# The up product of an MLP by seven half-size products (Strassen's scheme), one token block at a time, in a one-core encoder step on Trainium2

## The chip, the cores and the metric

The kernel runs on one core of one Trainium2 chip. A core has a matrix engine (TensorE, in the profile PE, with its weight loads as PEld), a vector engine (VectorE, DVE), an engine for functions of one input (ScalarE, ACT), a slower general engine (GpSimd, POOL) and an engine that issues DMAs (SyncE, SP). Each runs its own instruction stream in order and waits for the others by semaphores. The metric is the device time of one execution in microseconds (us); the time of a kernel is the median of its runs.

## What is computed

One step of a one-layer streaming encoder: 2048 prompt tokens and 32 sample tokens, model width 1024. A normed input goes through one projection, two kinds of attention, an output projection, then an MLP with squared ReLU and a gated per-layer input; last a norm. The part that matters here, from the reference:

```python
def ffn_ple(h, p, g_mlp, w_up, w_down, w_ple_gate, w_ple_proj):
    c = rmsnorm(h, g_mlp)
    h = h + jnp.square(jax.nn.relu(c @ w_up)) @ w_down
    return h + jax.nn.sigmoid(h @ w_ple_gate) * (p @ w_ple_proj)
...
        hp = hp + merge(oa, ob, subln_g[i], out_norm_b[i], w_out[i], lam_init)
        hp = ffn_ple(hp, p_prompt[i], g_mlp[i], w_up[i], w_down[i], w_ple_gate[i], w_ple_proj[i])
```

`w_up` is 1024 x 4096, `w_down` 4096 x 1024, `w_ple_gate` 1024 x 1024, `w_ple_proj` 256 x 1024, all float32.

## The kernel before

**Tokens.** They are held transposed (features on the 128 partitions, tokens along the free side) in four blocks of 512; the 32 sample tokens join block 3, which so has 544 and is computed in two halves of 272 (`SUBS`), since a matmul takes at most 512 columns.

**Split operands.** Every float32 operand `x` of a product is split into a rounded `hi` and a rest `lo = x - hi` (`split`, L167: ACT copies to `hi`, POOL or DVE subtracts for `lo`), and `mm3` (L191) makes three matmuls for each 128 x 128 weight tile: hi x hi, hi x lo, lo x hi. POOL's part goes through `pool_tt` (L148), which cuts a tensor into instructions of at most 256 columns. `wunit` (L178) loads 128 x 1024 weights into a raw tile and splits them whole; three such units are buffered.

**MLP of blocks 2 and 3.** `mlp` (L1033) runs 16 chunks of 256 hidden features. For a chunk, `mlp_up` (L973) loads two units of `w_up`, and for each of the two 128-feature tiles and each block makes 8 x 3 matmuls over the 1024 inputs into one PSUM bank, then ReLU, square and a split into `uh`, `ul` (two ACT passes L996 and L997, `hi` on ACT, `lo` on POOL). `mlp_down` (L1001) multiplies the outputs of the chunk before with two units of `w_down` and adds each PSUM result to `h` on DVE (L1031). Both blocks share each weight unit. Per chunk TensorE makes 48 up matmuls of 512 columns and 96 of 272, and as many down matmuls.

**Around it.** Blocks 0 and 1 go first. The second part of `run` (from L1316) then runs: `outproj(2)`; `outproj(3)` with `cnorm(2)` (the normed and split MLP input of block 2, L925) woven in; `gate(0)` (L1048) with `cnorm(3)` woven in; the final norm of block 0 behind the first chunk of the MLP; the MLP of blocks 2 and 3; `gate(2)`; `gate(3)` with `final(2)` in it; and `final(3)` (L1106), whose last half closes the run. A gate splits `h` into eight tiles (`hu` or `hH`, `hL`), makes for each of eight output tiles 24 gate matmuls (`gps`) and 6 projection matmuls (`pps`) per block of columns, computes a sigmoid on ACT with a subtraction on POOL, multiplies on DVE and adds to `h` on POOL.

**Order.** The kernel is written in Python generators that are woven by hand (`weave`, `drain`, `next`); this sets priorities. A planner then lists the instructions of each engine by these priorities and a model of their times, so that the matmuls of up and down products stand interleaved in TensorE's stream. Buffers are tiles of pools with a number of slots per name; an instruction that needs a slot waits for its last reader.

## Time and profile before

| | |
|---|---|
| median of 3 runs | 3222.55 us |
| lowest and highest run | 3216.17 and 3224.60 us |
| the profiled execution, whole | 3219.67 us |
| its span on the core | 3217.9 us |
| its mean granted TensorE clock | 0.981 |

The span runs from the first to the last instruction of the program; the rest of the execution's time lies around it. In the profile, a row of a group has the line, the engine, the operation, what it writes and reads, the shapes and the count; then busy time and the mean duration of one; then the idle time of that engine just before these instructions and what ended it. A row of the timeline has the start in us from the beginning of the span and the duration; in square brackets stands the idle time before it. Matmuls overlap in the pipeline, so their durations are longer than the distance between two starts.

### The profile page before, as it was taken

To read this page: it belongs to the slowest core of one execution; us is meant where nothing else is said; L and a number is where in the kernel's file an instruction comes from. 1 tells how busy PE (TensorE), PEld (TensorE's weight loads), DVE (VectorE), ACT (ScalarE), POOL (GpSimd) and SP (SyncE) were. 2 spreads that over 40 slices of the span, in tenths; PEclk is the share of its full clock that TensorE was granted. 3 is DMA by queue.
4 is the path that set the end of the run, shared out by engine and by line. 5 is a ranking of instruction groups with operands and counts; after the bars stand their busy time and mean duration, and the time that the engine had idled before them with its cause. 6 is when DMAs were issued, how large, how long until landed. Compare 5 with 4: busy or idle time off the path is not lost. (4 is left out here: it accounts for less than half of the span.)

```text
span 3217.9 us, 51221 instructions
## 1 busy us (share of the span) xinstructions
PE 3073.5 (96%) x17881; PEld 2698.6 (84%) x17881; DVE 1560.4 (48%) x3969; ACT 1724.7 (54%) x3819; POOL 1704.1 (53%) x2530
## 2 busy tenths in 40 slices
PE   8998989999999998999999999999999999999998
PEld 7787877899987787878788888888789999999988
DVE  5156774544465554676755656526432223223335
ACT  6256775766675674766666666444542322322255
POOL 4466546434345544565655545687954433333387
PEclk9998999999999999999999999999999999999999
DMA  8787768976787645555564543548431111111122
GB/s 265 238 245 222 204 193 235 258 221 203 204 247 221 202 126 144 151 154 149 154 180 126 141 120 107 158 124 259 145 111 44 45 47 47 46 47 47 59 86 87
DMA packets 503273, 487.90 MB, mean 152 GB/s; under 512 B 36924, under 2 KB 392576, under 8 KB 503016
## 3 DMA queue, kind: packets, MB, share of 16 engines
q1 hardware_dynamic: 503016, 484.64, 51.5%
q8 instruction: 141, 2.31, 0.3%
q14 instruction: 116, 0.95, 0.1%
HBM read 378.52 MB, written 109.95 MB: 152 GB/s over the span
## 5 line engine op out<-in xcount | busy, mean ns | idle before, releaser
L165 POOL TENSOR_TENSOR wl<-wr,wh 128x256 fp32r<-128x256 f32 x936 | 689.1, 768 | 466.2 <-ACT wh L170 454.2
L170 ACT ACTIVATE wh<-wr 128x1024 fp32r<-128x1024 f32 x338 | 357.0, 1057 | 590.8 <-PE dps L196 291.5
L1031 DVE TENSOR_TENSOR h<-h,dps 128x512 f32<-128x512 f32 (+1 forms) x640 | 373.8, 586 | 584.8 <-PE dps L197 567.8
L155 POOL TENSOR_TENSOR wl<-wr,wh 128x256 fp32r<-128x256 f32 x416 | 308.5, 772 | 359.7 <-ACT wh L170 354.2
L195 PE MATMUL dps<-uh,wh 128*128 128x512 f32 (+1 forms) x1280 | 458.4, 358 | 21.9 <-ACT wh L170 7.8
L196 PE MATMUL ups<-cL,wh 128*128 128x512 f32 (+1 forms) x1280 | 451.4, 353 | 2.0 <-POOL cL L155 1.8
L195 PE MATMUL ups<-cH,wh 128*128 128x512 f32 (+1 forms) x1280 | 451.7, 353 | 0.5 <-DVE h L1031 0.4
L196 PE MATMUL dps<-ul,wh 128*128 128x512 f32 (+1 forms) x1280 | 451.1, 353 | 0.0
L197 PE MATMUL ups<-cH,wl 128*128 128x512 f32 (+1 forms) x1280 | 451.0, 352 | 0.0
L197 PE MATMUL dps<-uh,wl 128*128 128x512 f32 (+1 forms) x1280 | 450.5, 353 | 0.0
L195 PEld LDWEIGHTS dps<-uh,wh 128*128 128x128 f32 x1280 | 241.9, 189 | 57.6 <-DVE h L1031 12.8
L155 POOL TENSOR_TENSOR ul<-relu,uh 128x136 fp32r<-128x136 f32 (+1 forms) x320 | 198.0, 640 | 170.9 <-ACT uh L170 169.7
L197 PEld LDWEIGHTS dps<-uh,wl 128*128 128x128 f32 x1280 | 241.3, 189 | 33.3
L196 PEld LDWEIGHTS ups<-cL,wh 128*128 128x128 f32 x1280 | 241.6, 189 | 32.8 <-POOL cL L155 2.0
L195 PEld LDWEIGHTS ups<-cH,wh 128*128 128x128 f32 x1280 | 241.6, 189 | 32.8 <-DVE h L1031 1.6
L197 PEld LDWEIGHTS ups<-cH,wl 128*128 128x128 f32 x1280 | 241.6, 189 | 29.4
L196 PEld LDWEIGHTS dps<-ul,wh 128*128 128x128 f32 x1280 | 242.0, 189 | 26.7
L195 PE MATMUL qps<-aH,wh 128*128 128x512 f32 (+1 forms) x640 | 230.0, 359 | 5.7 <-DVE ql L455 4.2
L196 PE MATMUL qps<-aL,wh 128*128 128x512 f32 (+1 forms) x640 | 228.6, 357 | 0.0
L197 PE MATMUL qps<-aH,wl 128*128 128x512 f32 (+1 forms) x640 | 228.3, 357 | 0.0
L612 PE MATMUL s<-ka,q 128*128 128x512 f32 (+3 forms) x768 | 188.1, 348 | 20.9 <-DMA ka<-kS 8.5
L626 ACT ACTIVATE e<-s,nm 128x512 f32<-128x512 f32 (+3 forms) x256 | 154.8, 609 | 75.6 <-DVE nm L618 64.5
(233 smaller groups left out, 7160.8 us busy)
## 6 DMA issues: line engine op xcount, KB each, us to landing
wr<-w_up SPq DMA_DIRECT2D x96, 512.0 KB, 4.1
wr<-w_down SPq DMA_DIRECT2D x96, 512.0 KB, 3.8
wr<-w_in SPq DMA_DIRECT2D x74, 512.0 KB, 4.7
q<-qS SPq DMA_DIRECT2D x128, 256.0 KB, 5.6
v<-vSa SPq DMA_DIRECT2D x64, 512.0 KB, 3.7
ka<-kS SPq DMA_DIRECT2D x32, 512.0 KB, 7.9
wr<-w_out SPq DMA_DIRECT2D x32, 512.0 KB, 4.9
wr<-w_ple_gate SPq DMA_DIRECT2D x32, 512.0 KB, 4.2
```

The lines of the kernel that those rows point to most:

```text
L155: nc.gpsimd.tensor_tensor(out[:, sl], a[:, sl], b[:, sl], op=op)
L165: nc.gpsimd.tensor_tensor(out[:, sl], a[:, sl], b[:, sl], op=op)
L170: nc.scalar.activation(hi, raw, AF.Copy)
L195: nc.tensor.matmul(ps, lh, rh, start=start and i == 0, stop=False)
L196: nc.tensor.matmul(ps, lh, rl, start=False, stop=False)
L197: nc.tensor.matmul(ps, ll, rh, start=False, stop=stop and i == n - 1)
L612: nc.tensor.matmul(s, q[:, m, hl, P * qi : P * qi + nr], kt[:, m, k0 - kb : k0 - kb + n], start=hl == 0, stop=hl == 1)
L626: nc.scalar.activation(dst, src, AF.Exp, bias=nmx, accum_out=z[:nr, m, bi : bi + 1])
L1031: nc.vector.tensor_tensor(hv, hv, ps, op=ALU.add)
```

## The change

For blocks 2 and 3 the up product of a chunk is taken as a product of 2 x 2 blocks: the weights are cut into two halves of hidden features (128 each) and two halves of inputs (512 each), the tokens into two halves (256 each, or 272 in block 3). Seven half-size products of sums of these parts replace the eight (the Winograd form of Strassen's scheme). `cparts` builds the seven token-side operands once per block (seven hi/lo pairs, in four steps); `mlp7` builds the seven weight-side operands per chunk and adds the products up on DVE, ACT and POOL. `mlp7` takes one block, so the MLP runs as 16 chunks for block 2 and then 16 for block 3; each loads and splits its weights itself. `gate(2)` now stands between them, with `cparts(3)` woven in; `cparts(2)` is woven into `gate(0)`, where `cnorm(3)` was. Weights after block 1 are split in pieces of 512 columns with eight piece buffers (`pieces`). At the end, the two POOL steps of the last two output tiles of `gate(3)` go to DVE, and in the last norm half of the scalings go to ACT. Cut to its core:

```diff
+class Parts:
+    def __init__(self, tiles, per):
+        self.tiles, self.per = tiles, per
+    def __getitem__(self, idx):
+        k = idx[1]
+        return self.tiles[k // self.per][(idx[0], k % self.per) + tuple(idx[2:])]
...
@@ wunit
+        if self.pieces is not None:
+            n = shape[0] // 2
+            parts = []
+            for x in range(2):
+                parts.append(self.piece([n] + shape[1:]))
+                self.split(*parts[x], raw[:, n * x : n * x + n], hi_eng, lo_eng)
+            return tuple(Parts([p[i] for p in parts], n) for i in range(2))
...
+    def piece(self, shape):
+        return [r.tile([P] + shape, F32R, name="piece") for r in self.pieces]
...
+    def cparts(self, b, wk, cs, out, r):
...
+        names = ("b11", "b21", "t2", "t1", "t3", "b22", "t4")
+        ops = {x: [cs.tile([P, 4, 272], F32R, tag="cs", name="cs")[:, :, :m] for _ in range(2)] for x in names}
+        for k in range(4):
+            c = []
+            for i in range(2):
+                tmp = wk.tile([P, BLK], F32, tag="tmp", bufs=self.nt, name="tmp")[:, :n]
+                kk = k + 4 * i
+                self.dma(tmp, self.hS[:, kk, t0 : t0 + n])
+                nc.vector.scalar_tensor_tensor(
+                    tmp, tmp, self.g_mlp[:, kk : kk + 1], r, op0=ALU.mult, op1=ALU.mult
+                )
+                c.append((tmp[:, :m], tmp[:, m:]))
+            (b11, b12), (b21, b22) = c
...
+            parts(("b11", "pool"), ("b21", "dve"), ("b22", "pool"))
+            nc.vector.tensor_tensor(b22, b22, b12, op=ALU.subtract)
+            nc.vector.tensor_tensor(b12, b12, b11, op=ALU.subtract)
+            nc.vector.tensor_tensor(b11, b22, b11, op=ALU.add)
+            nc.vector.tensor_tensor(b21, b21, b11, op=ALU.subtract)
+            parts(("t2", "dve"), ("t1", "pool"), ("t3", "dve"), ("t4", "pool"))
+            yield
...
+    def mlp7(self, b, h, ops, wk, up, mm, md):
...
+        def downs(ch, us):
+            for dh in range(2):
+                wh, wl = self.wunit(
...
+                for d in range(4):
+                    for s0, sn in SUBS[b]:
+                        ps = md.tile([P, 512], F32, tag="mm", name="dps")[:, :sn]
...
+                        nc.vector.tensor_tensor(hv, hv, ps, op=ALU.add)
+                    yield
...
+        def prod(out, more, w, x):
+            ps = banks.tile([P, 512], F32, name="ups")[:, :m]
+            self.mm3(ps, [(w[0][:, k], w[1][:, k], ops[x][0][:, k], ops[x][1][:, k]) for k in range(4)])
+            if more is None:
+                nc.scalar.activation(out, ps, AF.Copy)
+            else:
+                nc.vector.tensor_tensor(out, more, ps, op=ALU.add)
+            return out
+
+        def square(u, r, lo_eng):
+            nc.scalar.activation(r, r, AF.Relu)
+            nc.scalar.activation(r, r, AF.Square)
+            self.split(*u, r, "act", lo_eng)
...
+        for ch in range(DFF // (2 * P)):
...
+            self.split(*w["a11"], a11)
+            self.split(*w["a12"], a12)
+            s2 = self.sums.tile([P, 4, P], F32, tag="s2", bufs=1, name="s2")
+            nc.vector.tensor_tensor(a21, a11, a21, op=ALU.subtract)
+            nc.vector.tensor_tensor(s2, a22, a21, op=ALU.subtract)
+            nc.vector.tensor_tensor(a11, s2, a11, op=ALU.add)
+            nc.vector.tensor_tensor(a12, a12, s2, op=ALU.subtract)
+            for x, t, e in (("s2", s2, "dve"), ("s1", a11, "pool"), ("s3", a21, "dve"), ("s4", a12, "pool"), ("a22", a22, "dve")):
+                self.split(*w[x], t, "act", e)
...
+            t1 = prod(tmp("t1", m), None, w["a11"], "b11")
+            prod(c11, t1, w["a12"], "b21")
+            u2 = prod(tmp("u2", m), t1, w["s2"], "t2")
+            next(prev, None)
+            t5 = prod(tmp("t5", m), None, w["s1"], "t1")
+            next(prev, None)
+            u3 = prod(tmp("u3", m), u2, w["s3"], "t3")
+            self.pool_tt(u2, u2, t5, ALU.add)
+            self.pool_tt(c22, u3, t5, ALU.add)
+            next(prev, None)
+            next(prev, None)
+            prod(c12, u2, w["s4"], "b22")
+            square(us[0], r0, "dve")
+            next(prev, None)
+            prod(c21, u3, w["a22"], "t4")
+            square(us[1], r1, "pool")
+            drain(prev)
+            prev = downs(ch, us)
+            yield
+        drain(prev)
...
@@ gate
-                    self.pool_tt(sg, sm, sg, ALU.subtract)
+                    end = b == 3 and d >= 6
+                    if end:
+                        nc.vector.tensor_tensor(sg, sm, sg, op=ALU.subtract)
+                    else:
+                        self.pool_tt(sg, sm, sg, ALU.subtract)
...
-                    self.pool_tt(hv, hv, sg, ALU.add)
+                    if end:
+                        nc.vector.tensor_tensor(hv, hv, sg, op=ALU.add)
+                    else:
+                        self.pool_tt(hv, hv, sg, ALU.add)
@@ final
-                nc.vector.tensor_copy(yns[c0, q][:tn], yp[:tn])
+                if phased:
+                    nc.vector.tensor_tensor(yns[c0, q][:tn], yp[:tn], self.gf[:tn, :512], op=ALU.mult)
+                else:
+                    nc.vector.tensor_copy(yns[c0, q][:tn], yp[:tn])
...
-                nc.vector.scalar_tensor_tensor(yn[:tn], src[:tn], r, g, op0=ALU.mult, op1=ALU.mult)
+                if phased and q == 0:
+                    nc.scalar.activation(yn[:tn], src[:tn], AF.Copy, scale=r)
+                else:
+                    nc.vector.scalar_tensor_tensor(yn[:tn], src[:tn], r, g, op0=ALU.mult, op1=ALU.mult)
@@ run
+            wpx.close()
+            self.wp = opened(top, "wp4", 6)
+            wx = opened(top, "wx", 2, side="right")
+            self.sums = wx
+            self.pieces = [Rings(*[(self.wp, t)] * 3, (wx, t)) for t in ("wh", "wl")]
...
+            cs = Sized(opened(top, "cs", 14), None)
+            ops = {}
+            h = hload(hh, BLK, 0)
+            g = self.gate(0, h, up, None, md, wk)
             next(g)
...
-            r = self.colnorm(acc[3][0], 3, 1.0 / D, wk, mm, "mm", None)
-            weave(g, self.cnorm(3, wk, act, cn, r), 1)
+            r3 = self.colnorm(acc[3][0], 3, 1.0 / D, wk, mm, "mm", None)
+            weave(g, self.cparts(2, wk, cs, ops, r2), 1)
             f = self.final(0, h, up, fk, mm)
-            st = {b: (hload(hh, BLK, b),) + cn[b] for b in HALVES[1]}
-            m = self.mlp(HALVES[1], st, wk, up, mm, md)
+            h = hload(hh, BLK, 2)
+            m = self.mlp7(2, h, ops[2], wk, up, mm, md)
             next(m)
             drain(f)
             drain(m)
-            drain(self.gate(2, st[2][0], up, act, md))
-            g = self.gate(3, st[3][0], up, act, md)
-            f = self.final(2, st[2][0], up, fk, mm)
-            for _ in range(4):
+            g = self.gate(2, h, up, None, md, wk)
+            next(g)
+            weave(g, self.cparts(3, wk, cs, ops, r3), 1)
+            f = self.final(2, h, up, fk, mm)
+            h = hload(hh, BLK, 3)
+            m = self.mlp7(3, h, ops[3], wk, up, mm, md)
+            next(m)
+            drain(f)
+            drain(m)
+            g = self.gate(3, h, up, cs, md)
+            f = self.final(3, h, up, fk, mm, md)
+            for _ in range(5):
                 next(g)
...
```

More of the change, by code (lines that the diff above doesn't have):

```diff
@@ L139, in __init__ @@
         self.nt = 3
+        self.pieces = None
     def dma(self, dst, src):
@@ L941, in cnorm, with parts @@
             yield
+    def cparts(self, b, wk, cs, out, r):
+        nc = self.nc
+        n, t0 = BN[b], 512 * b
+        m = n // 2
+        names = ("b11", "b21", "t2", "t1", "t3", "b22", "t4")
+        ops = {x: [cs.tile([P, 4, 272], F32R, tag="cs", name="cs")[:, :, :m] for _ in range(2)] for x in names}
+        out[b] = ops
+        for k in range(4):
[9 more added lines that the diff above has]
+            (b11, b12), (b21, b22) = c
+            raw = {"b11": b11, "b21": b21, "b22": b22, "t3": b22, "t1": b12, "t2": b11, "t4": b21}
+            def parts(*which):
+                for x, e in which:
+                    self.split(ops[x][0][:, k], ops[x][1][:, k], raw[x], "act", e)
+            parts(("b11", "pool"), ("b21", "dve"), ("b22", "pool"))
[5 more added lines that the diff above has]
+            yield
     def colnorm(self, *args):
@@ L1055, in gate @@
                 self.dma(pT[i][k][:, :n], self.pS[:, i, k, t0 : t0 + n])
-        if wk is None:
+        if wk is None and act.aw is None:
+            hc = [act.tile([P, 4, 272], F32R, tag="cs", name="hc").rearrange("p a b -> p (a b)") for _ in range(8)]
+            hH, hL = [[hc[4 * i + k // 2][:, BLK * (k % 2) : BLK * (k % 2) + n] for k in range(8)] for i in range(2)]
+        elif wk is None:
             hH = act.tile([P, 8, act.aw], F32R, tag="act", name="hH")
```

63 lines of the change are left out of this document (50 added, 13 removed).

## The prediction

> **What bounds the kernel now.** I read the page first, then the last third of the span in stretches, then the timeline of TensorE and of POOL in it.
>
> ```profile
> span 3217.9 us, 51221 instructions
> PE 3073.5 (96%) x17881; PEld 2698.6 (84%) x17881; DVE 1560.4 (48%) x3969; ACT 1724.7 (54%) x3819; POOL 1704.1 (53%) x2530
> PE   8998989999999998999999999999999999999998
> POOL 4466546434345544565655545687954433333387
> ```
>
> TensorE never rests from the 30th slice on, and POOL is at three to four tenths in the MLP of blocks 2 and 3 but at eight or nine around it (the gates). By stretches (columns: length; busy us and instructions of PE, PEld, DVE, ACT, POOL; clock; DMA):
>
> ```profile
> 2264.00:2327.00 63.00, 59.16 (x245) 46.68 (x246) 31.34 (x36) 34.35 (x55) 58.78 (x80) 0.97 0.45 137
> 2327.00:2362.00 35.00, 32.62 (x194) 29.15 (x193) 11.85 (x17) 18.54 (x38) 30.81 (x45) 0.95 0.29 92
> 2362.00:3079.00 717.00, 716.03 (x4447) 649.90 (x4446) 213.06 (x417) 207.12 (x365) 281.62 (x442) 1.00 0.17 53
> 3079.00:3200.00 121.00, 120.67 (x764) 109.65 (x763) 46.43 (x90) 68.39 (x148) 102.83 (x165) 1.00 0.28 88
> ```
>
> The rows are gate(0), the MLP's start, the rest of the MLP, and gates 2 and 3. The MLP is bound by TensorE alone (0.97 us idle in 717), so fewer matmul columns there shorten the run, as long as the other engines keep up.
>
> **What a matmul costs.** Busy times overlap, so I use the distance between starts: in a run of 512-column matmuls, one of 272 and one of 256 (value projection, early in the kernel).
>
> ```profile
> 3086.24 0.40 PE L195 MATMUL gps<-hH,wh 128*128 128x512 f32 x1
> ...
> 3089.93 0.39 PE L196 MATMUL gps<-hL,wh 128*128 128x512 f32 x1
> ```
> ```profile
> 2601.24 0.29 PE L195 MATMUL ups<-cH,wh 128*128 128x272 f32 x1
> ...
> 2603.99 0.28 PE L196 MATMUL ups<-cL,wh 128*128 128x272 f32 x1
> ```
> ```profile
> 51.79 0.28 PE L195 MATMUL vps<-wh,aH 128*128 128x256 f32 x1
> ...
> 54.09 0.28 PE L197 MATMUL vps<-wh,aL 128*128 128x256 f32 x1
> ```
>
> 3.69 us over 16 steps is 0.231 us; 2.75 over 22 is 0.125; 2.30 over 20 is 0.115 (its first five steps are 0.12). As a check, one third at 0.231 and two thirds at 0.125 give 0.160 us; the MLP row has 717/4447 = 0.161. So halving a 512-column matmul, each half with its own weight load, costs almost nothing. I take 0.1165 for 256 columns, bounds 0.115 and 0.120.
>
> The page "TensorE: Matmul & The Clock Gate" of the Trainium skill, section "Back-to-back issue gap", speaks against the change: it gives a sustained spacing of about 131 ns at 512 columns and 81 at 128. An estimate between them is 98 ns at 256, so 1344 x 98 - 768 x 131 ns would add 31 us in block 2 instead of removing 20. The rows above contradict it at both widths.
>
> **The terms.** Up product of block 2, 16 chunks: before 16 x 48 = 768 matmuls of 512, 177.4 us; after 16 x 7 x 4 x 3 = 1344 of 256, 156.6: -20.8 (bounds -16 and -23). Block 3: before 16 x 96 = 1536 of 272, after 1344 of 272: 192 x 0.125 = -24.0. Down products, gates and transposes keep their matmuls. **Sum on TensorE: -44.8.**
>
> What is added is vector work: each block now loads and splits its own weights, the up weights become seven pieces, and products are summed outside PSUM. Prices:
>
> ```profile
> L155 POOL TENSOR_TENSOR wl<-wr,wh 128x256 fp32r<-128x256 f32 x132 | 93.2, 737 | 173.7 <-ACT wh L170 173.7
> L155 POOL TENSOR_TENSOR ul<-relu,uh 128x136 fp32r<-128x136 f32 x128 | 58.4, 477 | 33.1 <-ACT uh L170 33.1
> L170 ACT ACTIVATE uh<-relu 128x272 fp32r<-128x272 f32 x64 | 27.6, 432 | 2.0
> L170 ACT ACTIVATE uh<-relu 128x512 fp32r<-128x512 f32 x32 | 20.2, 632 | 1.0
> L1031 DVE TENSOR_TENSOR h<-h,dps 128x272 f32<-128x272 f32 x254 | 110.6, 438 | 50.0 <-PE dps L197 38.0 <-DMA h<-hS 3.8
> L1031 DVE TENSOR_TENSOR h<-h,dps 128x512 f32<-128x512 f32 x128 | 88.0, 688 | 452.6 <-PE dps L197 452.4
> ```
>
> Per chunk of block 2, TensorE needs 84 x 0.1165 + 48 x 0.231 = 20.9 us. ACT: 11 pieces, 6 passes of the two squares at 0.632, two copies at 0.43: 11.6. POOL: lo halves of four up pieces and four down pieces (two instructions each), two sums, two for a square's lo half: 20 x 0.737 = 14.7. DVE: 8 x 0.688 down sums, 5 x 0.438 product sums, and eight 512-wide instructions with both inputs in SBUF (four weight sums, four lo halves). Those eight decide, because they and POOL get in each other's way (the down sums, with one input in PSUM, leave POOL at 737 ns above):
>
> ```profile
> 2212.07 4.73 POOL L165 TENSOR_TENSOR wl<-wr,wh 128x256 fp32r<-128x256 f32 x4
> ```
> ```profile
> 2311.62 5.61 DVE L937 SCALAR_TENSOR_TENSOR tmp<-tmp,g_mlp_s,r 128x544 f32<-128x544 f32 x1 [0.73 <-DMA tmp<-hS]
> 2317.95 0.72 DVE L176 TENSOR_TENSOR cL<-tmp,cH 128x544 fp32r<-128x544 f32 x1 [0.72 <-ACT cH L170]
> ```
>
> Four POOL instructions, one DVE instruction beside each, took 4.73 us instead of 4 x 0.737: each DVE instruction adds 0.45 to POOL. The other way a DVE instruction waited 5 us behind POOL's; behind it would stand the product and down sums, whose eight PSUM banks TensorE wants back after eight groups of 12 x 0.1165 or 6 x 0.231 = 1.4 us, so 11 us of cover. The Trainium skill ("SBUF — State Buffer", section "Who interferes with whom") says that a DVE instruction with two SBUF inputs contends with one of GpSimd that reads SBUF, and that the shared pair is an exclusive lock. The trace agrees on the contention, but with 0.45 us of delay and not the full 0.72.
>
> So POOL's path is 14.7 + 8 x 0.45 = 18.3 us per chunk against 20.9 (88%). Block 3: 16 x 0.737 + 4 x 0.477 + three thirds of a 544-wide row (about 0.575 each, between the two rows) = 15.4, with 3.6 of delay 19.0 against (84 + 96) x 0.125 = 22.5. DVE is 7.7 + 8 x 1.17 = 17.1 us with its waits. Everything fits, but the eight piece buffers for eleven pieces per chunk leave little slack: the first down pieces of a chunk get their buffers as the last chunk ends, and TensorE wants them 3 products, 4.2 us, later; two pieces need about 0.63 + 4 x 0.737 = 3.6. The **stall in the steady chunks** is unknown: 0 as in the present MLP, or up to 8 x (0.72 - 0.45) = 2.2 us each if POOL waits out each DVE instruction whole. I take 0.3, near the row of the MLP, which is the nearest: **+10** over 32 chunks.
>
> **The stage borders.** Building the seven operand parts (cparts) is woven into gate(0) and now also into gate(2), which stood free. A gate is 240 x 0.231 = 55.4 us of TensorE and about 80 POOL instructions (40 weight lo's, 8 for h, 32 of sigmoid and sum): 59.0 us. Gate(2) gets 32 of 136 columns (15.3) and from DVE 12 wide and 28 half instructions (12 x 0.45 + 28 x 0.23 = 11.8): 86 us. Work ahead in the eight pieces is 16 instructions (11.8), and the last two columns' sums (5.9) can trail: 68 - 55.4 = 13 us of stall, where the row of gates 2 and 3 shows 0.3 now: **+13** (bounds 4, if the planner spreads the sums into the MLP, and 28). Gate(0): 59.0 + 16 x 0.737 + 11.8 = 82.6, less 17.7, less 55.4: 9.5, where the first two stretch rows show 6.2 idle, and the MLP's start offers less cover (9.8 us of products in chunk 0 instead of 23): **+6** (bounds 0 and 14). Gate(2)'s lo halves share 20 tiles with the MLP's outputs, of which the last four come free at its end: **+1**. The operands' DMAs and the second reading of the up and down weights cost nothing while the DMA share is 0.17; doubled it stays below the 0.45 of gate(0), and a load lands in a fifth of a chunk; uncovered, each would cost those 4 us:
>
> ```profile
> wr<-w_up SPq DMA_DIRECT2D x96, 512.0 KB, 4.1
> ```
>
> **The tail.** After the last gate matmul:
>
> ```profile
> 3200.25 0.29 PE L197 MATMUL gps<-hH,wl 128*128 128x272 f32 x1
> ...
> 3201.98 0.91 POOL L155 TENSOR_TENSOR sig<-sm,sig 128x136 f32<-128x136 f32 x2 [0.93 <-ACT sig L1085]
> ...
> 3204.02 0.90 POOL L155 TENSOR_TENSOR h<-h,sig 128x136 f32<-128x136 f32 x2 [1.14 <-DVE sig L1101]
> ```
> ```profile
> 3208.49 0.75 DVE L1143 SCALAR_TENSOR_TENSOR yn<-yn,rsy,gf 128x512 f32<-128x512 f32 x1
> ...
> 3214.44 0.73 DVE L1143 SCALAR_TENSOR_TENSOR yo<-yp,rsy,gf 32x512 f32<-32x512 f32 x1
> ```
>
> The two POOL steps go to DVE: 2 x (0.9 - 0.44) = -0.9. The ten scalings of 0.66 in a row become five on DVE and five on ACT side by side: -3.3. **-4** together (0 if ACT waits for DVE's lock, -5 at best).
>
> **Sum:** -44.8 - 4 + 10 + 13 + 6 + 1 = -19. The profiled execution took 3219.67 us (its span and 1.8 around it), 2.9 under the median of the runs; so 3201 from it, 3204 from the median. I predict **3202**.
>
> **Rivals.**
>
> *The shared path binds the chunk (slower).* If each of the eight DVE instructions holds POOL for its full 0.72 us, POOL's path is 14.7 + 5.8 = 20.5 us of 20.9, and the order of waits does the rest: late lo halves hold the piece buffers, the next raw loads and the down products. For it: the 5.6 us wait above, and DVE at 17 us. Against it: gate(0) ran 63 us with POOL at 58.78 busy and TensorE lost 3.8. Without steady stalls the sum is -29, so the sign turns at 0.9 us per chunk; at 2 us it is +35: 3256.
>
> *A draw.* Stalls of 0.6 to 1.2 us per chunk, with borders as forecast, eat the gain: -29 + 32 x 0.6 to -29 + 32 x 1.2 is -10 to +9, about 3222.
>
> *The borders cost nothing.* The order of instructions pushes POOL's gate sums into the MLP, as now at 2327 (30.81 of 35 us POOL busy while TensorE ran 32.62), and steady chunks run full: -44.8 - 4 + 4 = -45: 3176. Against it: the MLP that follows has no longer 60% of POOL free, but 12%.
>
> *The matmul count saves nothing*, since a half-width matmul is bound by its weight load: the 256-column run speaks against it. At 0.132 per matmul block 2 gains nothing: -19 + 21: 3222.
>
> **How the numbers follow.** Forecast 0.48, draw 0.10, shared path 0.27, free borders 0.13, weight load 0.02. About 0.3% (9.7 us) is what a measurement here can tell from no change: the forecast is faster but for its upper edge (0.44 of 0.48), free borders are faster; that is 0.57. Same: 0.04 + 0.10 + 0.02 = 0.16. Slower: 0.27. The forecast's own range is 3186 to 3216 (steady 0 to 0.5 us, borders within their bounds); the range to both rivals is 3174 to 3256.
>
> **What would show it.** Right: up products of block 2 start every 0.115 to 0.12 us, the two MLPs have TensorE idle under 1% with POOL near 75 to 80% busy, gate(2) is 10 us or more longer than 55 with TensorE waiting for the lo halves of weights or operand parts, and the tail from the last gate matmul is 13 to 14 us instead of 17.6. Wrong: PE waits for POOL or DVE in every chunk (shared path), a gate(2) without idle time, or a pitch of 0.13 and more. The prediction falls if either MLP has over 15 us of TensorE idle.

## The result, and the profile after

| | before | after |
|---|---|---|
| median of 12 runs each | 3218.45 us | 3225.85 us |
| lowest and highest | 3213.31 and 3224.60 us | 3217.70 and 3229.67 us |
| the profiled execution, its span | 3219.67, 3217.9 us | 3225.84, 3224.0 us |
| mean granted clock | 0.981 | 0.976 |

After over before is 1.002 (95% interval 1.001 to 1.0029): the changed kernel is 0.2% slower, some 6 us, where 0.5% faster was forecast. The page of the changed kernel, cut to four of its rows, shows that TensorE did get less to do:

```profile
PE 3036.1 (94%) x18265; PEld 2691.8 (83%) x18265; DVE 1854.1 (58%) x4436; ACT 1885.7 (58%) x4166; POOL 1959.8 (61%) x2782
PE   8998989999999999999999999999989999799998
POOL 4466556433345444665555545678977778877675
PEclk9998999999999999999999999999999999899999
```

PE's busy time fell from 3073.5 to 3036.1 us, 37 less, and the span still grew by 6.1. The unbroken row of nines from the 30th slice on has two dents now, an 8 in the 30th slice and a 7 in the 35th, and in the latter the granted clock has one too. POOL went from three or four tenths to seven or eight. The stretches show which stages the dents are in. The columns are the length, then busy us and instructions of PE, PEld, DVE, ACT and POOL, the clock, the DMA share and GB/s. Before, the start of `outproj(2)`, the MLP of both blocks, and gates 2 and 3:

```profile
2158.80:2160.60 1.80, 1.80 (x11) 1.45 (x9) 0.00 (x0) 1.58 (x3) 0.72 (x2) 1.00 0.40 121
...
2326.90:3079.30 752.40, 749.05 (x4642) 679.41 (x4641) 225.07 (x433) 225.96 (x403) 312.83 (x488) 1.00 0.18 55
3079.30:3200.50 121.20, 120.87 (x765) 109.85 (x764) 46.33 (x89) 68.09 (x148) 102.89 (x165) 1.00 0.28 88
```

After, the start of `outproj(2)` (from the last gate matmul of block 1 to the first `ops`), both output projections, gate(0), block 2's MLP, gate(2) with block 3's MLP, gate(3), and the tail:

```profile
2157.80:2169.70 11.90, 5.26 (x25) 3.77 (x23) 4.90 (x8) 5.22 (x13) 3.07 (x5) 0.75 0.84 264
2169.70:2272.90 103.20, 97.88 (x590) 87.54 (x591) 47.64 (x74) 45.55 (x92) 86.46 (x113) 0.98 0.78 233
2272.90:2336.00 63.10, 58.15 (x246) 46.66 (x245) 50.21 (x61) 36.81 (x77) 59.10 (x69) 0.97 0.32 97
2336.00:2695.10 359.10, 346.30 (x2145) 309.52 (x2144) 235.31 (x375) 188.00 (x350) 275.07 (x346) 0.99 0.36 112
2695.10:3145.30 450.20, 426.32 (x3152) 413.44 (x3151) 300.23 (x558) 224.93 (x421) 348.93 (x483) 0.97 0.32 99
3145.30:3206.80 61.50, 61.50 (x494) 61.50 (x493) 19.69 (x43) 34.76 (x84) 45.23 (x84) 1.00 0.13 35
3206.80:3224.00 17.20, 3.64 (x31) 2.99 (x29) 6.56 (x15) 9.01 (x24) 0.00 (x0) 0.74 0.36 130
```

The MLPs with their gates took 752.4 + 121.2 = 873.6 us and take 359.1 + 450.2 + 61.5 = 870.8. The whole scheme of seven products thus bought 2.8 us, and the start of `outproj(2)` alone costs 10.1 more than before (11.9 against 1.8). Inside the two MLPs, away from their starts, all is as it should be. Stretches of the changed kernel: the start of block 2's MLP, its steady part, gate(2), the start of block 3's MLP, its steady part:

```profile
2336.00:2400.00 64.00, 51.20 (x334) 45.95 (x333) 49.06 (x85) 34.78 (x82) 52.74 (x64) 0.92 0.44 151
2400.00:2690.00 290.00, 290.00 (x1792) 259.45 (x1791) 181.15 (x283) 148.91 (x261) 217.92 (x278) 1.00 0.34 105
2695.00:2766.00 71.00, 58.74 (x250) 47.24 (x249) 49.37 (x55) 35.89 (x74) 65.18 (x90) 0.90 0.31 91
2766.00:2830.00 64.00, 52.76 (x400) 51.70 (x399) 47.53 (x94) 33.75 (x79) 51.98 (x67) 0.92 0.35 116
2830.00:3145.00 315.00, 314.62 (x2506) 314.29 (x2505) 203.13 (x410) 155.27 (x267) 231.57 (x328) 1.00 0.32 98
```

In the steady parts TensorE idles 0.00 of 290 and 0.38 of 315 us; all the idle time lies in the other three rows (12.8, 12.3 and 11.2 us). What TensorE waited for there, the three longest rows in the list of its waits from 2100 us on (us in total, times, longest):

```profile
PE dps L215 <- ACT uh L180: 15.6, 2, 9.5
PE pps L215 <- DVE sm L1237: 11.8, 2, 6.9
PE ups L215 <- ACT cs L180: 5.4, 1, 5.4
```

The first row is the start of both MLPs (6.1 and 9.5 us): down products that wait for the first squared `uh`. In the second row 4.9 us belong to gate(0) and 6.9 to gate(2), to which the third row belongs as well. Gate(2)'s timeline on TensorE (start, duration, in brackets the idle time before):

```profile
2753.87 0.59 PE L215 MATMUL ups<-cs,piece 128*128 128x272 f32 x1 [5.37 <-ACT cs L180]
2761.36 0.79 PE L215 MATMUL pps<-pT,piece 128*128 128x512 f32 x1 [6.89 <-DVE sm L1237]
2761.95 0.63 PE L216 MATMUL pps<-pT,piece 128*128 128x512 f32 x1
2762.38 0.63 PE L217 MATMUL pps<-pT,piece 128*128 128x512 f32 x1
...
2766.37 0.40 PE L217 MATMUL gps<-hu,piece 128*128 128x512 f32 x1
```

Two waits of 5.4 and 6.9 us: block 3's products had already begun while the gate's last column waited for its vector work, then ran out of operand parts. The last gate matmul starts at 2766.4, so gate(2) took 71.3 us from 2695.1. And where TensorE comes back from such a stall it is slow: 512-column matmuls start 0.43 us apart at 2762, where they start 0.23 apart elsewhere. Stretches laid along the slow clock, in block 2's start, in gate(2) and in block 3's start:

```profile
2354.90:2365.10 10.20, 5.52 (x22) 5.23 (x23) 5.42 (x7) 5.11 (x11) 10.20 (x14) 0.50 0.47 154
2750.90:2764.50 13.60, 3.74 (x8) 2.77 (x9) 12.22 (x17) 7.48 (x17) 9.97 (x15) 0.50 0.12 39
2785.00:2795.20 10.20, 4.08 (x18) 4.08 (x19) 3.58 (x5) 4.71 (x9) 9.84 (x16) 0.50 0.48 144
```

A mean of 0.50 means half clock throughout.

### The profile page after: what moved, and what is told of

It is laid out like the page before. It is cut to its first block, busy times and chain, and to the rows that moved or that the text cites. A ratio compares the mean times of both kernels' runs of the same rounds, so it can differ in the third digit from the quotient of the medians.

```text
span 3224.0 us, 53645 instructions
## 1 busy us (share of the span) xinstructions
PE 3036.1 (94%) x18265; PEld 2691.8 (83%) x18265; DVE 1854.1 (58%) x4436; ACT 1885.7 (58%) x4166; POOL 1959.8 (61%) x2782
## 3 DMA queue, kind: packets, MB, share of 16 engines
q14 instruction: 129, 1.06, 0.1%
## 4 chain that ended last, share of the span: by engine, by line
PE 53%; DMA 4%; DVE 4%; POOL 2%; ACT 2%; issue 1%; SPq 0%; DVEq 0%; ACTq 0%; POOLq 0%
PE dps L215 7%; PE dps L216 7%; PE dps L217 7%; PE ups L215 6%; PE ups L216 6%; PE ups L217 6%; PE s L632 2%; PE gps L216 1%; PE gps L215 1%; PE gps L217 1%; PE tpp L704 1%; DMA wr<-w_up 1%; DMA tmp<-hS 1%; POOL piece L175 1%; PE ops L215 1%
## 5 line engine op out<-in xcount | busy, mean ns | idle before, releaser
L175 POOL TENSOR_TENSOR wl<-wr,wh 128x256 fp32r<-128x256 f32 x648 | 473.7, 762 | 328.9 <-ACT wh L180 318.4
L180 ACT ACTIVATE piece<-wr 128x512 fp32r<-128x512 f32 x412 | 254.0, 627 | 310.8 <-PE ups L216 160.5
L175 POOL TENSOR_TENSOR piece<-wr,piece 128x256 fp32r<-128x256 f32 x416 | 334.3, 828 | 119.2 <-ACT piece L180 106.4
L165 POOL TENSOR_TENSOR wl<-wr,wh 128x256 fp32r<-128x256 f32 x264 | 198.8, 783 | 182.1 <-ACT wh L180 176.8
L215 PE MATMUL ups<-cs,piece 128*128 128x256 f32 (+1 forms) x896 | 256.9, 287 | 10.3 <-ACT cs L180 5.4
L215 PE MATMUL dps<-uh,piece 128*128 128x272 f32 (+1 forms) x768 | 247.1, 327 | 16.0 <-ACT uh L180 15.6
L217 PE MATMUL ups<-cs,piece 128*128 128x256 f32 (+1 forms) x896 | 256.7, 287 | 0.6 <-POOL piece L175 0.6
L216 PE MATMUL ups<-cs,piece 128*128 128x256 f32 (+1 forms) x896 | 256.0, 286 | 0.5 <-DVE cs L186 0.5
L216 PE MATMUL dps<-ul,piece 128*128 128x272 f32 (+1 forms) x768 | 247.9, 324 | 0.4 <-DVE ul L186 0.4
L217 PE MATMUL dps<-uh,piece 128*128 128x272 f32 (+1 forms) x768 | 247.2, 324 | 0.0
L165 POOL TENSOR_TENSOR piece<-wr,piece 128x256 fp32r<-128x256 f32 x280 | 223.1, 830 | 15.6 <-ACT piece L180 15.1
L215 PE MATMUL dps<-uh,wh 128*128 128x512 f32 x512 | 209.9, 410 | 21.3 <-ACT wh L180 7.4
L632 PE MATMUL s<-ka,q 128*128 128x512 f32 (+3 forms) x768 | 187.7, 347 | 22.5 <-DMA ka<-kS 12.1
L215 PE MATMUL ups<-cH,wh 128*128 128x512 f32 x512 | 202.7, 396 | 0.5 <-DVE h L1083 0.4
L216 PE MATMUL dps<-ul,wh 128*128 128x512 f32 x512 | 202.7, 396 | 0.0
L217 PE MATMUL dps<-uh,wl 128*128 128x512 f32 x512 | 202.3, 395 | 0.0
```

The source lines that it names most:

```text
L165: nc.gpsimd.tensor_tensor(out[:, sl], a[:, sl], b[:, sl], op=op)
L175: nc.gpsimd.tensor_tensor(out[:, sl], a[:, sl], b[:, sl], op=op)
L180: nc.scalar.activation(hi, raw, AF.Copy)
L215: nc.tensor.matmul(ps, lh, rh, start=start and i == 0, stop=False)
L216: nc.tensor.matmul(ps, lh, rl, start=False, stop=False)
L217: nc.tensor.matmul(ps, ll, rh, start=False, stop=stop and i == n - 1)
```

## The experiments

Each experiment's ratio is to the kernel before on the same chip, whose median there stands beside it; the medians of one kernel differ between chips, so that across groups only ratios are compared. A ratio is estimated from all runs of both kernels and so differs from the quotient of the two medians by up to 0.07%. "The change" has 1.002, taken to hold on every chip. The first four ask where the borders lose.

**Reopening the weight pool alone, on the kernel before.**

```diff
-            self.wp = opened(top, "wp", 3)
+            wpx = ExitStack()
+            self.wp = opened(wpx, "wp", 3)
...
+            wpx.close()
+            self.wp = opened(top, "wp4", 3)
```

> The kernel before, with one thing of the change alone: the weight pool is closed and opened again ahead of outproj(2), at the same size. Theory (borders): the first w_out load can no longer be issued while gate(1) runs, since its buffer overlaps the closed pool's; in the changed kernel the first ops matmul came 11.9 us after the last gps matmul, before 1.8. Expected here: a gap of 10 to 12 us and +8 to +10 us in time (3227). Rival (the gap belongs to the 512-column pieces, not to the pool): gap about 2 us, time within 3 us of before.

3220.66 against 3219.27 us, ratio 1.0008 (0.9996 to 1.0021). TensorE at the start of `outproj(2)`:

```profile
2155.56 0.39 PE L197 MATMUL gps<-hH,wl 128*128 128x512 f32 x1
...
2161.06 0.50 PE L195 MATMUL ops<-ou,wh 128*128 128x512 f32 x1 [1.42 <-ACT wh L170]
```

5.5 us instead of 1.8, ended by a weight split (`wh` on ACT) that comes late. That is 3.7 of the 10.1 us; the expected 10 to 12 us gap didn't come, so reopening is part of it and not all. Nor is it the part that was expected: the load of `w_out` that was to be late starts at 2141.49, while gate(1) still runs (2144.74 before). What comes late is its split, first before and then here:

```profile
2152.18 1.06 ACT L170 ACTIVATE wh<-wr 128x1024 fp32r<-128x1024 f32 x1 [2.19 <-PE gps L196]
...
2159.97 2.94 ACT L170 ACTIVATE wh<-wr 128x1024 fp32r<-128x1024 f32 x3
```

**Raw tiles kept, in the changed kernel.** The raw tiles go to a pool of their own, opened once at the top.

```diff
+            rw = opened(top, "rw", 2)
...
-            self.rawp = Rings((self.wp, "wr"))
+            self.rawp = Rings((rw, "wr"))
...
-            self.rawp = Rings((self.wp, "wr"), (wk, "wr"))
+            self.rawp = Rings((rw, "wr"), (wk, "wr"))
```

> The changed kernel, with the raw weight tiles in a pool of their own that stays open for the whole kernel, so that only the split pieces' pool is reopened. Theory (the late w_out load makes the gap ahead of outproj(2)): the first two loads are issued during gate(1), the gap of 11.9 us falls to 2 to 4, time -8 to -10 us against the change: 3216 to 3218. Rival (the pieces' buffers themselves come free late): gap over 8 us, time within 3 us of the change.

3218.98 against 3219.27 us, ratio 0.9999 (0.9987 to 1.001), 0.21% under the change, some 7 us. The transfers in SP's queue, in the changed kernel:

```profile
2158.19 0.56 SPq L156 DMA_DIRECT2D h<-hS  x1
2158.87 15.45 SPq L156 DMA_DIRECT2D wr<-w_out  x4
```

With raw tiles kept, SP's queue and then TensorE:

```profile
2141.77 6.36 SPq L156 DMA_DIRECT2D wr<-w_out  x2
...
2158.10 0.50 PE L215 MATMUL ops<-ou,piece 128*128 128x512 f32 x1
```

The loads of `w_out` start 17 us earlier, ahead of the end of gate(1) instead of behind it, and the gap is 2.3 us (from 2155.8). With that the start of `outproj(2)` is explained by the late loads, and these by where the raw tiles lie. How the pool holds the loads back is not shown: in the changed kernel SP's queue waited 19.3 us for the last gate matmul with the load of `h`, and the loads of `w_out` stand right behind it, so they may have had to wait for memory of the closed pool themselves, or only for their turn.

**Gate sums on DVE.** In gates 0 and 2, which pass `wk`, the two POOL steps of each output tile go to DVE.

```diff
-                    end = b == 3 and d >= 6
+                    end = wk is not None or (b == 3 and d >= 6)
```

> The changed kernel, with the sigmoid's subtraction and the sum into h of gate(0) and gate(2) on DVE instead of POOL (32 POOL instructions of 0.74 us per gate become 16 of DVE). Theory (POOL's backlog at the gates starves TensorE and then the first chunks of the MLP): POOL loses 23.6 us per gate, gate(2) falls from 71 us to 60 or less, the stalls of the first 60 us of both MLPs (12.8 and 10.8 us idle) shrink by half or more: 20 to 30 us faster than the change, 3197 to 3206. Rival (the two engines' shared path is full, so moving work from one to the other gains nothing): DVE busy rises to over 60 of the 71 us and the time stays within 5 us of the change's 3225.9.

3213.92 against 3219.27 us, ratio 0.9981 (0.9966 to 0.9996), 0.39% under the change, some 12.5 us. Stretches of the start of the first MLP, gate(2), and the start of the second:

```profile
2330.00:2394.00 64.00, 49.63 (x319) 45.03 (x318) 53.54 (x97) 38.40 (x87) 42.94 (x49) 0.89 0.43 149
2692.00:2749.00 57.00, 55.84 (x241) 44.83 (x240) 43.18 (x60) 32.12 (x66) 51.27 (x63) 1.00 0.35 106
2749.00:2813.00 64.00, 53.69 (x377) 51.03 (x376) 55.24 (x106) 38.92 (x88) 47.26 (x59) 0.92 0.36 121
```

Gate(2) falls from 71 to 55.5 us and idles 1.2: POOL was what stretched it. But the MLPs' starts still idle 14.4 and 10.3 of 64 us, with DVE at 53.5 and 55.2, so less was gained than the expected 20 to 30 us. The gates were cured; the starts weren't.

**POOL's share of block 3's operand parts left out.** Four `lo` halves of `cparts(3)` that POOL makes are left out, and other `lo` tiles are read in their place.

```diff
+        if b == 3:
+            for x, y in (("b11", "b21"), ("b22", "t2"), ("t1", "t3"), ("t4", "b21")):
+                ops[x] = [ops[x][0], ops[y][1]]
...
+                    if b == 3 and e == "pool":
+                        nc.scalar.activation(ops[x][0][:, k], raw[x], AF.Copy)
+                        continue
```

> The changed kernel, with the four lo halves that POOL makes in cparts of block 3 left out (other lo tiles are read in their place): 32 POOL instructions of 136 columns less, 15.3 us, all in gate(2). Theory (cparts(3) on POOL is what stretches gate(2)): gate(2) from 71 to about 60 us, and part of the 10.8 us idle after it goes: 10 to 18 us faster than the change, 3208 to 3216. Rival (gate(2) waits for DVE's chain of sums and loads, not for POOL): under 5 us faster.

3213.22 against 3219.27 us, ratio 0.9987 (0.9976 to 0.9998), 0.33% under the change, some 11 us. Gate(2) and the start after it:

```profile
2694.00:2749.00 55.00, 55.00 (x238) 44.43 (x237) 40.82 (x52) 31.67 (x66) 52.47 (x59) 1.00 0.37 116
2749.00:2813.00 64.00, 52.92 (x374) 50.81 (x373) 49.88 (x95) 37.90 (x88) 47.80 (x61) 0.92 0.33 108
```

Gate(2) doesn't idle at all, and the start of the second MLP does as before (11.1 against 11.2). So the stall of gate(2) is POOL's queue, as forecast, and the start has a cause of its own.

**Both cures together** (gate sums on DVE and raw tiles kept; the two diffs above).

> The changed kernel with both of the edits that helped: gate sums of gate(0) and gate(2) on DVE, and the raw weight pool kept open. Theory (two separate border losses, one ahead of outproj(2), one at the gates): the gains add, -7 and -12.5 us: 3206, some 0.4% under the kernel before. Rival (one hides the other, since both free the same stretch of POOL work ahead): 3212 to 3214, no better than either alone.

3199.36 against 3213.64 us, ratio 0.9961 (0.9947 to 0.9976). The single effects, -0.39% and -0.21%, on 1.002 give 0.996: they add. This is already faster than either kernel. A stretch at the start of block 2's MLP, then DVE's groups there (2313 to 2375; busy, mean ns), then two rows of SP's queue:

```profile
2313.00:2335.00 22.00, 16.46 (x103) 15.33 (x102) 20.93 (x32) 14.30 (x29) 15.19 (x16) 0.77 0.16 51
```
```profile
L1310 DVE SCALAR_TENSOR_TENSOR yn<-yn,rsy,gf 128x512 f32<-128x512 f32 x8 | 7.0, 920 | 0.1
L1289 DVE COPY yn<-yp 128x512 f32<-128x512 f32 x8 | 5.4, 682 | 0.3 <-PE yp L1281 0.2
```
```profile
2347.93 12.21 SPq L156 DMA_DIRECT2D y_prompt<-yn  x4
2362.59 1.71 SPq L156 DMA_DIRECT2D wr<-w_up  x2
```

DVE is full, 20.93 of 22 us. In this first stretch 6.0 us of it are the gate's trailing subtractions and sums, which this version gave to DVE. The final norm of block 0, which is drained behind the first chunk, follows: 12.4 us up to 2375, of which 8.3 in the 20 us from 2355 on. Its stores also stand ahead of loads of `w_up` in SP's queue.

The next three are on top of this version.

**Operand parts two steps per gate column.**

```diff
-            weave(g, self.cparts(2, wk, cs, ops, r2), 1)
+            weave(g, self.cparts(2, wk, cs, ops, r2), 1, 0, 2)
...
-            weave(g, self.cparts(3, wk, cs, ops, r3), 1)
+            weave(g, self.cparts(3, wk, cs, ops, r3), 1, 0, 2)
```

> As e5_gate_and_raw, but two steps of cparts after each gate column and not one, so the operand parts are ready by the fourth of eight columns. Theory (the MLP's first product waits for the last operand parts, which come after the gate): the waits of ups for cs (6 us in the gate-sums run) go, 4 to 8 us faster than e5. Rival (the MLP's start waits for its weights: raw load, four sums, seven pieces in a row): the same time within 3 us, the idle time moves to waits for pieces and for the square's uh.

3202.19 us, ratio 0.9964 (0.9952 to 0.9977): no gain. In the profiled execution the waits for `cs` are gone (6.3 us in the version it stands on), but gates 0 and 2 take 59.0 and 61.5 us instead of 54.7 and 55.5. The wait only moved.

**First chunk ahead of the gate's last two columns.**

```diff
-            weave(g, self.cparts(2, wk, cs, ops, r2), 1)
+            c = self.cparts(2, wk, cs, ops, r2)
+            for _ in range(5):
+                next(g)
+                next(c, None)
+            drain(c)
...
             next(m)
+            drain(g)
             drain(f)
```

(and the same for block 3.)

> As e5_gate_and_raw, but the first chunk of each seven-product MLP is put ahead of the last two gate columns, so its loads, sums and pieces are prepared while TensorE still has gate work. Theory (an MLP's start is a serial pipeline fill of load, sums, pieces, products, square, for which TensorE has no other work): the idle time in the 60 us after each gate (14 and 10 us with the gate sums on DVE) falls to half and fewer half-clock windows follow: 8 to 15 us faster than e5, 3191 to 3198. Rival (POOL and DVE are full in that stretch, so the gate's last columns come late instead): within 4 us of e5.

3208.63 against 3213.64 us, ratio 0.9987 (0.9977 to 0.9998): about 8 us worse than the version it stands on. The gates, which now hold the first chunk's products, stretch to 78 to 80 us, and in the 140 us from each gate's start TensorE is busy 125.2 and 123.5 us instead of 126.7 and 127.7. Moving the pipeline's fill forward only moves the vector work to where there is more of it; this idea fell.

**Stores of the last norm's first half issued by ACT.**

```diff
-                self.dma(dst[:, 512 * q : 512 * q + 512], yn[:tn])
+                if phased and q == 0:
+                    nc.scalar.dma_start(dst[:, 512 * q : 512 * q + 512], yn[:tn])
+                else:
+                    self.dma(dst[:, 512 * q : 512 * q + 512], yn[:tn])
```

> As e5_gate_and_raw, but in the last norm the five stores of the first halves are issued from ACT's queue, the others from SP's. Theory (in the changed kernel the ten stores bind the tail: issued one after another by SP, 3215.5 to 3221.4, while the scalings on ACT and DVE are done in 3.4 us): from the last scaling's start the tail shortens by about 2 us: 2 to 3 us faster than e5. Rival (issuing from ACT delays its own scalings by as much, or the landing of the last store decides): within 1 us.

3198.26 us, ratio 0.9958 (0.9945 to 0.9971), 1.1 us from the version it stands on and within its interval. The profile's store row (KB each, median us from issue to landing):

```profile
y_prompt<-yo SPq DMA_DIRECT2D x4, 256.0 KB, 4.2
```

In the changed kernel that median is 3.0, before 2.2. Issued closer together, the stores land later: in the profiled execution it is 18.1 us from the last gate matmul to the end, in the version it stands on 17.5. In all these tails the same 2.23 MB move at some 360 to 410 GB/s once they flow, which suggests, without a run that shows it, that the transfer sets the pace.

The next three take the work at the MLPs' starts away bit by bit.

**Final norms spread over the chunks, in the changed kernel.** The final norm of blocks 0 and 2 goes one token tile per chunk from the third chunk on.

```diff
-            drain(f)
-            drain(m)
+            next(m)
+            weave(m, f, 1)
```

(in both places.)

> The changed kernel with one edit: the final norm of block 0 and of block 2 no longer runs as a whole behind the MLP's first chunk, but one token tile per chunk from the third chunk on. Theory (the start of an MLP is bound by DVE, which was busy 39.5 of 42 us in two stretches of e5's start, 12.4 of 20 us of it in the norm, and by SP's queue, where the norm's stores stand ahead of the next w_up loads): the idle and half-clock time in the 80 us after each gate falls by a third or more, 6 to 12 us faster than the change. Rival (the start is a serial fill of load, sums, pieces, product, square, and the norm only fills its gaps): within 3 us of the change.

3210.89 against 3212.38 us, ratio 1.0002 (0.9992 to 1.0013), 0.18% under the change; the intervals overlap a little. (The 12.4 us of norm in 20 that the expectation names lie in 62; in those 20 they are 8.3, as shown above.) In the profile, taken of the slowest of the twelve runs (3223.87 us), the first MLP's start gained (TensorE 56.53 of 64 us instead of 51.20), the second's didn't. Gate(2) and that second start:

```profile
2690.00:2758.00 68.00, 58.47 (x250) 47.27 (x249) 46.26 (x56) 36.35 (x75) 65.86 (x87) 0.92 0.32 95
2758.00:2822.00 64.00, 48.78 (x359) 47.66 (x358) 41.37 (x62) 27.48 (x51) 49.84 (x71) 0.87 0.25 83
```

POOL is the gate's bound (65.86 of 68), and after it an up product waits 4.9 us for a piece from POOL. That its arrears reach into the start whatever DVE has to do fits this and the next run, but was not tested by itself.

**All of it together**: gate sums on DVE, raw tiles kept, ACT's stores, final norms spread.

> All edits that helped (gate sums on DVE, raw weight pool kept open, half of the last stores from ACT's queue) and the norm spread over the chunks. Theory: what e9 gains comes on top of 0.9958: ratio to before 0.992 to 0.994. Rival: as without the spread, 0.995 to 0.997.

3189.91 against 3212.38 us, ratio 0.993 (0.9918 to 0.9943): 0.7% or 22 us faster than before, the fastest here that computes the whole reference. The spread is worth 0.28% on the cured gates. Starts of the two MLPs, in the slowest of its six runs (3198.79 us):

```profile
2326.00:2390.00 64.00, 55.26 (x342) 50.07 (x341) 47.12 (x73) 36.49 (x69) 48.40 (x56) 0.92 0.28 90
...
2739.00:2803.00 64.00, 58.48 (x419) 56.41 (x418) 48.55 (x84) 34.80 (x65) 51.40 (x68) 0.92 0.29 90
```

8.7 and 5.5 us idle instead of 12.8 and 11.2 in the change; DVE has some room again. The tail is as long as with ACT's stores alone (18.1 us), so the trace shows no gain from these.

**Without the weight sums in the first chunks.** On top of that, the four sums of weights are left out in the first two chunks of each MLP; their pieces are taken from the raw parts.

```diff
...
+            if ch < 2:
+                s2 = a22
+            else:
                 nc.vector.tensor_tensor(a21, a11, a21, op=ALU.subtract)
                 nc.vector.tensor_tensor(s2, a22, a21, op=ALU.subtract)
                 nc.vector.tensor_tensor(a11, s2, a11, op=ALU.add)
                 nc.vector.tensor_tensor(a12, a12, s2, op=ALU.subtract)
```

> As e10_all_and_spread, but in the first two chunks of each seven-product MLP the four weight sums on DVE are left out (the pieces are taken from the raw parts instead): 16 DVE instructions less in all, and a shorter chain from the load to the first pieces. Theory (DVE's time and the chain of sums set the start): another 4 to 8 us faster. Rival (the start waits for the products' own chain: product, sum, ReLU, square, uh, and for piece buffers): within 2 us of e10.

3179.73 against 3212.38 us, ratio 0.990 (0.9888 to 0.9913): another 10 us by the medians for 16 DVE instructions of about 0.9 us left out. The same stretches:

```profile
2315.00:2379.00 64.00, 58.83 (x378) 53.25 (x377) 45.49 (x70) 37.15 (x69) 49.14 (x59) 0.95 0.28 91
...
2726.00:2790.00 64.00, 59.81 (x453) 58.62 (x452) 44.90 (x82) 37.37 (x69) 51.20 (x71) 0.97 0.30 97
```

5.2 and 4.2 us are idle now, 4.8 less. From gate(0)'s start to the end the two profiled executions differ by 5.8 us, so that only this much of the gain is placed; the rest of their difference lies ahead of gate(0), where the edit changes nothing. The chain from a load over the sums, their pieces, the products and the square to the first down product is shorter here, and DVE has less to do: which of the two gave the idle time back is not separated. More raw tiles at the start, so that loads of chunk 1 begin sooner, were not tried.

**The tail's edits alone, on the kernel before** (the two POOL steps of `gate(3)` to DVE, half of the last scalings to ACT, as in the change).

```diff
-                    self.pool_tt(sg, sm, sg, ALU.subtract)
+                    end = b == 3 and d >= 6
+                    if end:
+                        nc.vector.tensor_tensor(sg, sm, sg, op=ALU.subtract)
+                    else:
+                        self.pool_tt(sg, sm, sg, ALU.subtract)
...
-                nc.vector.scalar_tensor_tensor(yn[:tn], src[:tn], r, g, op0=ALU.mult, op1=ALU.mult)
+                if phased and q == 0:
+                    nc.scalar.activation(yn[:tn], src[:tn], AF.Copy, scale=r)
+                else:
+                    nc.vector.scalar_tensor_tensor(yn[:tn], src[:tn], r, g, op0=ALU.mult, op1=ALU.mult)
```

> The kernel before, with the tail of the change alone: the last two columns' gate sums of block 3 on DVE, and half of the last scalings on ACT. By the prediction: -4 us, and 13 to 14 us from the last gate matmul to the end. Rival, from the trace of the change: the ten stores now follow each other so closely that SP's issue (0.36 to 0.6 us each, 0.33 before) and their landing (2.5 to 3.0 us, 2.1 before) take the gain back: -0.3 to -1 us, 17 us from the last gate matmul to the end, no difference that the timing can tell.

3210.90 against 3211.67 us, ratio 1.0001 (0.9989 to 1.0014): nothing. The last gate matmul, and the first and the last store in SP's queue:

```profile
3192.39 0.29 PE L197 MATMUL gps<-hH,wl 128*128 128x272 f32 x1
...
3201.37 0.33 SPq L146 DMA_DIRECT2D y_prompt<-yn  x1
...
3206.61 0.57 SPq L146 DMA_DIRECT2D y_sample<-yo  x1
```

From the last gate matmul to the end of the span (3209.8) it is 17.4 us, where the kernel before has 17.65 (3200.25 to 3217.9). The first scaling starts 8.2 us after that matmul in both, and the first store is issued after 9.0 us in both. The scalings then end sooner (five take 3.2 us on ACT beside 3.4 on DVE, instead of 6.7 in a row), but from the first store to the end it is 8.4 us instead of 8.6: issue and landing of the stores take up the gain.

## Why the prediction was wrong

The forecast of -19 us failed at three steps: it had no time for the start of block 3's MLP (+12.6 us) and none for the start of `outproj(2)` (+10.1), and it took 4 us off a tail that became 0.2 shorter. The stages add up to the profiled difference. Before's starting point is 1.0 us later (2158.8 against 2157.8). With 4608 MLP matmuls before, at 717/4447 = 0.1612 us (the prediction's row), the MLP takes 742.9 us. After, block 3's 2880 at 315/2506 = 0.1257 take 362.0. Block 2's steady row can't be used that way, since it holds 1106 up and 686 down products where a chunk has 84 and 48; in it the mean distance between starts is 0.1184 us at 256 columns and 0.2326 at 512, which gives 16 x (84 x 0.1184 + 48 x 0.2326) = 337.7 us. What a stage took beyond its matmuls is its border:

| term | forecast | traces |
|---|---|---|
| MLP matmuls with steady stalls | -44.8 + 10 = -34.8 | 337.7 + 362.0 - 742.9 = -43.2 |
| gate(0) and start of block 2's MLP, last tiles | +6 + 1 | +0.8 and (359.1 - 337.7) - (752.4 - 742.9) = +11.9 |
| gate(2) | +13 | 71.3 - 55.4 = +15.9 |
| start of block 3's MLP | none | 450.2 - 362.0 - 71.3 - 4.3 = +12.6 |
| start of `outproj(2)` | none | 11.9 - 1.8 = +10.1 |
| tail | -4 | 17.2 - 17.4 = -0.2 |
| output projections, and what lay before | 0 | 103.2 - 104.0 - 1.0 = -1.8 |
| sum | -18.8 | +6.1 |

(The 4.3 are the transposes of block 2's final norm, which before lay in gates 2 and 3 and after in block 3's start: 121.2 less gate(3)'s 61.5 and a gate's 55.4.)

**The matmul price was right.** In the steady part, 256-column matmuls and then a 512-column one:

```profile
2499.91 0.28 PE L215 MATMUL ups<-cs,piece 128*128 128x256 f32 x1
...
2500.97 0.40 PE L215 MATMUL dps<-uh,piece 128*128 128x512 f32 x1
```

1.06 us over 9 steps is 0.118, against 0.1165 forecast; the 272-column rate of block 3 is 0.1257 against 0.125. The rival in which the weight load binds falls.

**The steady chunks held too, better than forecast.** TensorE idles 0.38 us in 605 us, with POOL busy 75 and 74% of the time, as forecast. The +10 for stalls did not come: -43.2 is 1.6 short of the -44.8 of the matmul count, and that is the pitch (21.1 us for a chunk of block 2 against 20.9, 22.6 against 22.5 for one of block 3, and before's pitch was slower than 0.160 as well). That this term was too high by 8.4 us was luck: it hid a quarter of what the other terms missed. The rival with 27%, the shared path binding every chunk, was wrong in its place: DVE and POOL do bind, but at the starts.

**Gate(2) was right in size and cause.** +15.9 against +13, and taking POOL's work away removes it (gate sums on DVE, block 3's parts left out).

**Missing term 1: block 3's MLP has a start of its own.** The prediction costed "the MLP's start" once, for block 2, and for block 3 only the gate ahead of it. But one MLP became two, and each must fill the chain from load to square while the gate's arrears, the parts, the final norm and its stores share DVE and SP's queue with it: 12.6 us that stood nowhere, most of it idle time (11.2 us in the first 64). Block 2's start, which had a term, was mis-sized for the same reason: +12.7 with gate(0) against +7. The forecast of 9.8 us of products as cover in chunk 0 counted TensorE's work, not the time until it may begin. On the cured gates, the runs without the final norm and then without the weight sums at the start shortened just this, from 11.2 us of idle time to 5.5 and 4.2 in block 3's. No run keeps both blocks in one MLP of seven products, so that the second start comes from the split is argued, and what holds the start in the end stays open.

**Missing term 2: `outproj(2)` starts behind a reopened pool.** The diff showed `wpx.close()` and a new pool, but no term of the prediction lies ahead of gate(0). It took the loads of the MLPs as free since the DMA share is low, and a share says nothing of when a load may start. The run with raw tiles kept gave back 9.6 of the 11.9 us of gap; reopening on the kernel before made 3.7, by late splits and not by late loads.

**The tail was mis-sized.** -4 was taken from DVE's and POOL's rows alone, -0.2 was measured. The two POOL steps (-0.9) were not on the path: in the run with the tail alone the first scaling starts 8.2 us after the last gate matmul, as before. The scalings got 3.3 us shorter as forecast, but behind them stand the stores, issued from 3201.37 to 3206.61 at up to 0.60 us each instead of 0.33, and 17.4 us were left as they were.

**And the price of idle time was too low in principle.** The prediction counted the waits. After them TensorE ran at half clock, so that a stall also slows the work behind it. In the three stretches shown and one more in gate(0) (2331.0 to 2334.4) TensorE was busy 16.7 us. At full clock the same matmuls take half as long, so by an estimate the half clock cost 8 us there, against 3 in the kernel before (6.6 us busy at half clock in gate(0) and the MLP). These 5 us are part of the borders in the table; most of each border is the wait itself.

Its own condition, over 15 us of TensorE idle in either MLP, was not met by the MLPs alone: 12.8 us in block 2's, and 11.6 in block 3's. With the gate woven into its start block 3's has 23.9.

## What to carry to other kernels

Saving matmuls pays in the steady state and is given back at the borders, so count the borders: a stage split in two has two starts, each of which pays the chain from the first load to the first result on engines that are still busy with the stage before. Where a diff closes and reopens a pool, ask which loads used to start ahead of that point. Before giving up such a change, move the other work away from the starts and keep the loads ahead of the borders: here that turned 0.2% slower into 0.7% faster, the seven products untouched.

## What was not expected of the hardware

- Around and after waits TensorE ran at a granted clock of 0.50, with 512-column matmuls 0.43 us apart instead of 0.23. In the changed kernel waits of 4.9, 6.1, 5.4 and 6.9, and 9.5 us brought stretches of 3.4, 10.2, 13.6 and 10.2 us. The Trainium skill ("TensorE: Matmul & The Clock Gate", section "Part 1: The HAM clock gate") states that the clock halves after an idle window of about 3.4 us and returns after as long a busy one. Stretches of one, three, four and three such windows agree with the length. The idle window does not agree: in the kernel before, a wait of 1.8 us was enough, and in the 3.4 us ahead of the half clock TensorE was busy 1.63 of them (2339.7 to 2343.1), so a wait shorter than the window can halve the clock.
- A store's issue on SP grew from 0.33 us (first) to 0.57 (last) in the run with the tail alone, where stores come closer together, and the median landing from 2.2 to 4.2 us between the kernel before and the one with ACT's stores.
